# A three-block fp32 model on one core: modulation vectors by rows, convolution taps from PSUM, and other moves in the first block

## The chip, the cores and the metric

The program runs on one core of one Trainium2 chip. The metric is the device time of one execution in microseconds (us); lower is better. Before the change the median of three runs is 3274.16 us (3274.14 to 3275.22).

## What is computed

Three blocks in a chain act on x, 512 tokens by 1024 features, all in fp32. Only the first block changes. Cut to what matters here:

```
m_x = (silu(c) @ w_mod + b_mod)            # six vectors of 1024: shift, scale, gate, shift, scale, gate
m_c = (silu(c_ctx) @ w_mod + b_mod)
hc  = modulate(ctx, m_c[0], m_c[1]);  hx = modulate(x, m_x[0], m_x[1])     # rmsnorm, scale, shift
px  = hx @ w_in                            # columns: recurrent input 1280, gelu gate 1280, u, v, two gates
xr  = depthwise conv over time, 4 taps, of (ctx part, x part)
y_lru = RG-LRU both ways over ctx + x, 5 heads of 256: r, i = sigmoid(xr @ wa), sigmoid(xr @ wx)
        a = exp(-c softplus(lam) r);  h = a h + sqrt(1 - a*a) (i xr);  forward + backward
y_r = gelu(px gate) * y_lru;   y_g = u * (w_s v + b_s)
merged = sigmoid(gate_r) * (y_r @ w_pr) + sigmoid(gate_g) * (y_g @ w_pg)
x = x + m_x[2] * (merged @ w_out)
x = x + m_x[5] * conv_ffn(modulate(x, m_x[3], m_x[4]))
```

The second block begins with `silu(c_2) @ w_ada + b_ada`, three more vectors of 1024, which the first block computes on the side.

## The kernel before

**Products.** Each fp32 product is made of three passes: weight and activation are both split into a rounded high part and a low rest, and `dense` issues high by high (L419), high by low (L420) and low by high (L422) into one PSUM bank; `dense_n` (L438 to L440) is the same with the roles swapped. Activations stand as features by tokens, 128 features to a tile and 512 tokens (256 for ctx) to a row.

**Weights.** `Stream` brings all large weights in chunks of eight 128x128 tiles (512 KB) in the order in which they are used. SP loads a chunk into `wst` (two buffers, L99), then ACT (L102) or DVE (L104) casts it to the high part `whi`, by the letter that `hi_pattern` has for the chunk ("a" is ACT, "v" is DVE), and DVE subtracts for the low part `wlo` (L107). `whi` and `wlo` have rings of six buffers: chunk n can be cast only when PE is through with chunk n − 6.

**Start (`block1`).** x and ctx are loaded, the first 2048 columns of w_mod go through PE as 32 tiles `wm` of 256 KB (`gemv` inside `block1`), and x and ctx are normed and modulated.

**Recurrent part (`lru`).** For each of five heads: the convolution's input product for the next head into two banks (px for x, pc for ctx), its four taps (`conv_taps`), and for either direction the gates (`gates`): products into a PSUM tile `pair`, tanh on ACT (L866), exp and tanh of a (L871, L872), a*a on DVE (L873), the square root on ACT (L879), and the scan along time on DVE (L884 forward, L887 backward). The taps first copy px and pc to SBUF on ACT (L836, L837) into tiles with zeroed borders (Pool memsets); the first tap is a DVE tensor_scalar (L841), the others DVE scalar_tensor_tensor operations. That operation is issued by a helper, so every one of them has line L549.

**Mixer (`mixer1`).** Four loops over output tiles: u (8, with the chunk products L950 to L955), t1 (8), yr (10) and the merge loop (8), then w_out in `final_stage`: four output tiles at full width, then the other four in halves of 256 tokens. Each is closed by an epilogue on DVE, `xh<-mm,gate,s` (out = PSUM times gate plus residual), which frees the PSUM bank. Four banks carry the tag "mm" and are used in turn.

**Modulation vectors on the side (`gemv`, `column`).** The other 32 column groups of w_mod and the 24 of w_ada are computed on DVE: 14 blocks of eight tiles 128x512 (256 KB, four buffers `gv`), each tile scaled by a column of silu(c) and added up (L687 and L549), and after each block four small matmuls with ones on PE (L673) that add over the partitions. The blocks stand between the output tiles of the t1, yr and merge loops.

**Bias matrices (`toeplitz`).** A small table is expanded to `tmat` in DRAM, 4 MB written by two transfers on SP's queue ahead of the u loop; the second block reads it.

The program is written with a tile scheduler, which sets the order of the instructions on each engine; an engine then runs its own in that order and waits for what each needs.

Of the kernel before, what the change touches and what calls it, by code (L numbers as in the profile page):

```python
# [11 lines left out]
AF = mybir.ActivationFunctionType  # L12
OP = mybir.AluOpType
# [3 lines left out]
P = 128  # L17
D = 1024
KD = D // P
T = 512  # L20
# [354 lines left out]
class Kernel:  # L375
# [299 lines left out]
    def gemv(self, new, src, nblk, cs, out, bias):  # L675

        nc = self.nc
        prev = None
        for b in list(range(nblk)) + [None]:
            acc = None  # L680
            if b is not None:
                acc = new()
                for k in range(KD):
                    st = new()
                    nc.sync.dma_start(st, src[b][k])
                    if k == 0:
                        nc.vector.tensor_scalar(acc, st, cs[:, 0:1], None, op0=OP.mult)  # L687
                    else:
                        self.stt(acc, st, cs[:, k:k + 1], acc, OP.mult, OP.add)
            if prev is not None:  # L690
                ps = self.sd()
                self.column(ps, prev)
                o = slice(4 * b - 4, 4 * b) if b is not None else slice(4 * nblk - 4, 4 * nblk)
                nc.vector.tensor_add(out[:, o], ps[:, :4], bias[:, o])
            prev = acc
            yield
# [5 lines left out]
    def block1(self, es):  # L702
        nc, S, ai, cp, mod = self.nc, self.S, self.ai, self.cpool, self.mod
        with ExitStack() as b1:
# [8 lines left out]
            with ExitStack() as st:  # L713
# [4 lines left out]
                S.hi_pattern = "v"  # L718
# [11 lines left out]
                cs2 = cs.rearrange("p (a k) -> p k a", a=2)  # L730

                def gemv(i, b, at={}):
# [3 lines left out]
                    for k in range(KD):  # L736
                        wm = self.t(p0, [P, T], "wm", bufs=12)
                        nc.sync.dma_start(wm, ai["wmod01"][i][k])
                        if i < 2 and k % 2 == 0:
                            j = 4 * i + k // 2  # L740
                            nc.sync.dma_start(x[j], ai["xT"][j])
                            nc.sync.dma_start(ctx[j], ai["ctxT"][j])
                            nx.square("q", j, FULL)
                            ncx.square("q", j, ncols)
# [38 lines left out]
                t = gemv(2, 1, {0: t, 2: columns})  # L783
# [4 lines left out]
            S.hi_pattern = "v"  # L788
# [6 lines left out]
    def lru(self, hx, hc, s1c):  # L795
# [8 lines left out]
        with ExitStack() as es:  # L804
# [25 lines left out]
            def conv_taps(m, px, pc, xr, xs):  # L830
                bx = self.t(p, [P, T + 4], "bx", bufs=2)
                bc = self.t(p, [P, TC + 4], "bc", bufs=2)
                for b, n in ((bx, T), (bc, TC)):
                    nc.gpsimd.memset(b[:, 0:2], 0.0)
                    nc.gpsimd.memset(b[:, n + 2:n + 3], 0.0)
                nc.scalar.copy(bx[:, 2:T + 2], px)  # L836
                nc.scalar.copy(bc[:, 2:TC + 2], pc[:, :TC])  # L837
                r = self.t(p, [P, TC + T + TC], "xr", bufs=4)
                for b, n, o in ((bc, TC, 0), (bx, T, TC)):
                    dst = r[:, o:o + n]  # L840
                    nc.vector.tensor_scalar(dst, b[:, 0:n], self.v("cw1", m), self.v("cb1", m),  # L841
                                            op0=OP.mult, op1=OP.add)
                    for j in range(1, 4):
                        self.stt(dst, b[:, j:j + n], self.v("cw1", 10 * j + m), dst, OP.mult, OP.add)
# [7 lines left out]
            def gates(h, d, xr, xs, y):  # L852

                ax, ac = xs.view(slice(TC, N)), xs.view(slice(0, TC))
                q = self.t(p, [P, 2, N], "q", bufs=1)
                aa, bb = [], []
                for mt in range(2):
# [15 lines left out]
                    nc.vector.tensor_mul(q[:, mt, :], a, a)  # L873
# [6 lines left out]
                for mt in range(2):  # L880
                    nc.vector.tensor_mul(bb[mt], bb[mt], q[:, mt, :])
                    f = q[:, mt, :]
                    if d == 0:
                        nc.vector.tensor_tensor_scan(f, aa[mt], bb[mt], 0.0, op0=OP.mult, op1=OP.add)  # L884
                        nc.vector.tensor_copy(y[mt], f[:, TC:N])
                    else:
                        nc.vector.tensor_tensor_scan(f[:, ::-1], aa[mt][:, ::-1], bb[mt][:, ::-1], 0.0,  # L887
                                                     op0=OP.mult, op1=OP.add)
                        nc.vector.tensor_add(y[mt], y[mt], f[:, 0:T])
# [15 lines left out]
            for h in range(5):  # L905
                y = [self.xh() if 2 * h + i < 8 else self.t(self.s0, [P, T], f"y{2 * h + i}") for i in range(2)]
                nr, ns = [], Act()
                for d in range(2):
# [4 lines left out]
                    gates(h, d, xr, xs, y)  # L913
# [12 lines left out]
    def mixer1(self, hx, ylru, vt):  # L926
        nc, ai, cp, mod, cs = self.nc, self.ai, self.cpool, self.mod, self.cs
        with ExitStack() as es:
# [9 lines left out]
            self.toeplitz(slot)  # L938
            yg = Act()
            for m in range(8):  # L940
                pu = self.mm()
# [17 lines left out]
            gn = lambda: self.t(s2, [P, T], "gv", bufs=4)  # L959
            gv = self.gemv(gn, ai["wmod25"], 8, cs, mod[:, 16:48], self.v("b_mod", 16, 32))  # L960
            t1 = []
            for m in range(8):
# [4 lines left out]
                nc.scalar.activation(tg, pg, AF.Tanh, scale=0.5)  # L967
                self.dense("w_pg", m * P, KD, [(pp, yg)])
# [4 lines left out]
            for m in range(10):  # L973
                pr = self.mm()
                self.dense("w_in", 1280 + m * P, KD, [(pr, hx)])
# [6 lines left out]
                if m == 0:  # L982
                    next(gv)
            cs2 = self.t(self.s0, [P, 8], "cs_2")
            nc.scalar.activation(cs2, self.v("c2", 0, 8), AF.Silu)
            gv = self.gemv(gn, ai["wada"], 6, cs2, self.ada, self.v("b_ada", 0, 24))
            mg = Act()
            for m in range(8):
                pg, pp = self.mm(), self.mm()
                if m < 7:  # L990
                    next(gv)
                self.dense("w_in", 4608 + m * P, KD, [(pg, hx)])
                tg = tt()
                nc.scalar.activation(tg, pg, AF.Tanh, scale=0.5)
                self.dense("w_pr", m * P, 10, [(pp, yr)])
# [94 lines left out]
    def toeplitz(self, alloc):  # L1090
# [4 lines left out]
        nc.sync.dma_start(tab, self.ai["t5"])  # L1095
        for i in range(2):
            oh = alloc()[:33, :320]
            nc.sync.dma_start(oh, self.ai["onehot"][i])
# [4 lines left out]
            nc.sync.dma_start(self.trow[:, i * 320:(i + 1) * 320], row)  # L1103
        self.tmat = self.t(self.dpool, [16, P, T], "tmat")
        for r in range(0, 16, 8):
            src = self.trow[r:r + 8, 0:T]
            if not isinstance(src, Mock):
                src = bass.AP(tensor=src.tensor, offset=src.offset + 127, ap=[[640, 8], [-1, P], [1, T]])
            nc.sync.dma_start(self.tmat[r:r + 8], src)
# [873 lines left out]
```

## Time and profile before

| | |
|---|---|
| median of three runs | 3274.16 us |
| the profiled execution | 3279.36 us |
| span of its records | 3277.6 us |
| mean granted clock of PE | 0.988 |
| matmuls | 15534, 97% of the span busy |
| bytes moved | 352.52 MB, 108 GB/s on average |

The profile gives for every engine the busy time, and for an engine that sat idle what released it. The parts of the program can be told apart by time: start 0 to 45 us, recurrent part to 237, u loop to about 350, t1 and yr loops to about 490, merge loop to about 600, w_out to about 640, and then the first block's FFN and the other two blocks, whose instructions the change leaves as they are.

### The profile page before, as it was taken

To read this page: it belongs to the slowest core of one execution; us is meant where nothing else is said; L and a number is where in the kernel's file an instruction comes from. 1 tells how busy PE (TensorE), PEld (TensorE's weight loads), DVE (VectorE), ACT (ScalarE), POOL (GpSimd) and SP (SyncE) were. 2 spreads that over 40 slices of the span, in tenths; PEclk is the share of its full clock that TensorE was granted. 3 is DMA by queue.
4 is the path that set the end of the run, shared out by engine and by line. 5 is a ranking of instruction groups with operands and counts; after the bars stand their busy time and mean duration, and the time that the engine had idled before them with its cause. 6 is when DMAs were issued, how large, how long until landed. Compare 5 with 4: busy or idle time off the path is not lost.

```text
span 3277.6 us, 40053 instructions
## 1 busy us (share of the span) xinstructions
PE 3187.5 (97%) x15534; PEld 2639.8 (81%) x15534; DVE 2035.1 (62%) x3160; ACT 1310.2 (40%) x2010; POOL 193.6 (6%) x268
## 2 busy tenths in 40 slices
PE   8999999999999999999999999999899999989998
PEld 4778788888888888888887888888877787878887
DVE  6997676588837756655787353333796747563334
ACT  4665232344424444333665233222543535342222
POOL 2100000100001000000000010000200012020001
PEclk9999999999999999999999999999999999999999
DMA  5114776423333232222232333333323131333331
GB/s 204 52 58 134 238 223 199 140 90 97 106 113 105 78 90 84 84 90 85 74 97 74 110 116 103 103 106 106 117 75 124 61 105 61 122 103 97 106 109 62
DMA packets 123108, 352.52 MB, mean 108 GB/s; under 512 B 13978, under 2 KB 28668, under 8 KB 122788
## 3 DMA queue, kind: packets, MB, share of 16 engines
q1 hardware_dynamic: 118612, 336.18, 32.6%
q0 software_dynamic: 4304, 13.77, 1.3%
q8 instruction: 122, 2.00, 0.2%
q14 instruction: 70, 0.57, 0.1%
HBM read 337.27 MB, written 16.82 MB: 108 GB/s over the span
## 4 chain that ended last, share of the span: by engine, by line
PE 80%; DVE 11%; DMA 3%; issue 3%; ACT 2%; SPq 0%; POOL 0%; ACTq 0%; DVEq 0%; POOLq 0%
PE mm L420 19%; PE mm L419 19%; PE mm L422 18%; PE sd L420 4%; PE sd L422 4%; PE sd L419 4%; PE mm L440 2%; PE mm L439 2%; PE mm L438 2%; DVE wlo L107 2%; DMA gv<-in_wmod 2%; DVE xh L549 1%; PE sd L495 1%; PE sd L496 1%; PE sd L497 1%
## 5 line engine op out<-in xcount | busy, mean ns | idle before, releaser
L107 DVE TENSOR_TENSOR wlo<-wst,whi 128x1024 fp32r<-128x1024 f32 x496 | 609.4, 1230 | 614.7 <-ACT whi L102 605.5
L102 ACT CAST whi<-wst 128x1024 fp32r<-128x1024 f32 x485 | 509.1, 1051 | 1174.8 <-PE mm L420 732.5
L420 PE MATMUL mm<-xh,whi 128*128 128x512 f32 (+1 forms) x2256 | 857.5, 381 | 16.0 <-DVE xh L549 11.9
L419 PE MATMUL mm<-xh,whi 128*128 128x512 f32 (+1 forms) x2256 | 857.2, 381 | 14.5 <-ACT xh L364 10.5
L422 PE MATMUL mm<-xh,wlo 128*128 128x512 f32 (+1 forms) x2256 | 849.7, 379 | 0.0
L420 PEld LDWEIGHTS mm<-xh,whi 128*128 128x128 f32 x2256 | 430.4, 191 | 94.6 <-DVE xh L549 16.1
L419 PEld LDWEIGHTS mm<-xh,whi 128*128 128x128 f32 x2256 | 429.8, 191 | 94.5 <-ACT xh L364 11.4
L422 PEld LDWEIGHTS mm<-xh,wlo 128*128 128x128 f32 x2256 | 428.3, 191 | 74.0 <-issue 2.9
L419 PE MATMUL sd<-xh,whi 128*128 128x512 f32 (+1 forms) x576 | 215.2, 374 | 0.0
L420 PE MATMUL sd<-xh,whi 128*128 128x512 f32 (+1 forms) x576 | 214.6, 372 | 0.0
L422 PE MATMUL sd<-xh,wlo 128*128 128x512 f32 (+1 forms) x576 | 214.5, 372 | 0.0
L420 PE MATMUL mm<-d,whi 128*128 128x512 f32 (+1 forms) x540 | 187.7, 348 | 0.0
L422 PE MATMUL mm<-d,wlo 128*128 128x512 f32 (+1 forms) x540 | 187.2, 347 | 0.0
L419 PE MATMUL mm<-d,whi 128*128 128x512 f32 (+1 forms) x540 | 187.1, 347 | 0.0
L438 PE MATMUL mm<-whi,xh 128*128 128x512 f32 x336 | 131.7, 394 | 6.1 <-DVE whi L104 3.1
L439 PE MATMUL mm<-wlo,xh 128*128 128x512 f32 x336 | 132.8, 395 | 0.6 <-DVE wlo L107 0.6
L440 PE MATMUL mm<-whi,xh 128*128 128x512 f32 x336 | 132.0, 394 | 0.0
L549 DVE SCALAR_TENSOR_TENSOR t<-t,vec,t 128x441 f32<-128x441 f32 (+2 forms) x176 | 122.7, 701 | 9.6 <-ACT t L1046 5.3
L419 PEld LDWEIGHTS sd<-xh,whi 128*128 128x128 f32 x576 | 109.5, 190 | 18.8
L420 PEld LDWEIGHTS sd<-xh,whi 128*128 128x128 f32 x576 | 109.2, 190 | 18.8
L422 PEld LDWEIGHTS sd<-xh,wlo 128*128 128x128 f32 x576 | 109.2, 190 | 18.7
L1510 DVE TENSOR_TENSOR t<-t,sd 128x512 f32<-128x512 f32 x44 | 30.2, 688 | 144.7 <-PE sd L422 141.1
(482 smaller groups left out, 5187.6 us busy)
## 6 DMA issues: line engine op xcount, KB each, us to landing
wst<-in_w SPq DMA_DIRECT2D x516, 512.0 KB, 3.6
gv<-in_wmod SPq DMA_DIRECT2D x64, 256.0 KB, 3.5
gv<-in_wada SPq DMA_DIRECT2D x48, 256.0 KB, 3.5
t<-xd POOLq DMA_DIRECT2D x40, 256.0 KB, 3.6
xd<-xh SPq DMA_DIRECT2D x72, 128.0 KB, 1.8
wm<-in_wmod SPq DMA_DIRECT2D x32, 256.0 KB, 5.0
tmat<-trow SPq DMA_DIRECT2D x2, 2048.0 KB
tp<-tmat SPq DMA_DIRECT2D x16, 256.0 KB, 2.6
```

The source lines that it names most:

```text
L102: self.after(nc.scalar.copy(hi, st))
L107: self.after(eng.tensor_sub(lo, st, hi.bitcast(FT)))
L419: mm(ps, wh, a.hi[k], start=(k == 0), stop=False)
L420: mm(ps, wh, a.lo[k], start=False, stop=False)
L422: mm(ps, wl, a.hi[k], start=False, stop=(k == K - 1))
L438: mm(ps, a.hi[k][:, s], wh, start=(k == 0), stop=False)
L439: mm(ps, a.hi[k][:, s], wl, start=False, stop=False)
L440: mm(ps, a.lo[k][:, s], wh, start=False, stop=(k == K - 1))
L495: mm(ps, l[0], r[0], start=start, stop=False)
L496: mm(ps, l[0], r[1], start=False, stop=False)
L497: mm(ps, l[1], r[0], start=False, stop=stop)
L549: self.nc.vector.scalar_tensor_tensor(out, in0, s, in1, op0=op0, op1=op1)
```

## The change

1. **Modulation vectors by rows.** w_mod and w_ada are stored transposed. One tile is 128 columns of the matrix by 1024 inputs (512 KB, two buffers `gv`), and one DVE tensor_tensor_reduce (L681 of the changed kernel) multiplies it by silu(c), held in all 128 partitions (`cb`, one buffer, loaded on Pool's queue, Silu on ACT), and adds along the row. 56 tiles take the place of 14 blocks of eight; the small matmuls go. Two tiles stand beside each output tile of the u loop from the second on, two in t1, one in yr, two in the merge loop.
2. **Taps from PSUM.** ACT writes the tap of weight index 2 straight from PSUM with scale and bias; the three others are DVE operations that read PSUM. The copies, the borders and the memsets go.
3. **Gates.** a*a becomes an ACT Square; the buffer q has three copies instead of one; the forward result is no longer copied, since the backward add reads it in q.
4. **Casts.** At the start all high parts are cast on ACT instead of DVE, in the recurrent part every second one.
5. **Start.** x and ctx are loaded behind the weight tiles 0, 2, 5, 7, 10, 12, 15 and 17 instead of every second one of the first 16; the norm's columns come later.
6. **Bias matrices.** All their transfers go to Pool's queue, and `tmat` is written in eight pieces, most of them in the yr loop.

```diff
-    def gemv(self, new, src, nblk, cs, out, bias):
+    def gemv(self, new, src, n, cb, out, bias):
 
         nc = self.nc
-        prev = None
-        for b in list(range(nblk)) + [None]:
-            acc = None
-            if b is not None:
-                acc = new()
-                for k in range(KD):
-                    st = new()
-                    nc.sync.dma_start(st, src[b][k])
-                    if k == 0:
-                        nc.vector.tensor_scalar(acc, st, cs[:, 0:1], None, op0=OP.mult)
-                    else:
-                        self.stt(acc, st, cs[:, k:k + 1], acc, OP.mult, OP.add)
-            if prev is not None:
-                ps = self.sd()
-                self.column(ps, prev)
-                o = slice(4 * b - 4, 4 * b) if b is not None else slice(4 * nblk - 4, 4 * nblk)
-                nc.vector.tensor_add(out[:, o], ps[:, :4], bias[:, o])
-            prev = acc
+        for j in range(n):
+            st = new()
+            nc.sync.dma_start(st, src[j])
+            nc.vector.tensor_tensor_reduce(out=st, in0=st, in1=cb, op0=OP.mult, op1=OP.add, scale=1.0, scalar=0.0,
+                                           accum_out=out[:, j:j + 1])
+            if j == n - 1:
+                nc.vector.tensor_add(out, out, bias)
             yield
...
-                S.hi_pattern = "v"
+                S.hi_pattern = "a"
...
+                at_x = (0, 2, 5, 7, 10, 12, 15, 17)
...
-                        if i < 2 and k % 2 == 0:
-                            j = 4 * i + k // 2
+                        if 8 * i + k in at_x:
+                            j = at_x.index(8 * i + k)
...
-                t = gemv(2, 1, {0: t, 2: columns})
+                t = gemv(2, 1, {0: t, 1: nx.warm, 5: columns})
...
-            S.hi_pattern = "v"
+            S.hi_pattern = "av"
...
             def conv_taps(m, px, pc, xr, xs):
-                bx = self.t(p, [P, T + 4], "bx", bufs=2)
-                bc = self.t(p, [P, TC + 4], "bc", bufs=2)
-                for b, n in ((bx, T), (bc, TC)):
-                    nc.gpsimd.memset(b[:, 0:2], 0.0)
-                    nc.gpsimd.memset(b[:, n + 2:n + 3], 0.0)
-                nc.scalar.copy(bx[:, 2:T + 2], px)
-                nc.scalar.copy(bc[:, 2:TC + 2], pc[:, :TC])
                 r = self.t(p, [P, TC + T + TC], "xr", bufs=4)
-                for b, n, o in ((bc, TC, 0), (bx, T, TC)):
-                    dst = r[:, o:o + n]
-                    nc.vector.tensor_scalar(dst, b[:, 0:n], self.v("cw1", m), self.v("cb1", m),
-                                            op0=OP.mult, op1=OP.add)
-                    for j in range(1, 4):
-                        self.stt(dst, b[:, j:j + n], self.v("cw1", 10 * j + m), dst, OP.mult, OP.add)
+                for ps, n, o in ((pc, TC, 0), (px, T, TC)):
+                    nc.scalar.activation(r[:, o:o + n], ps[:, :n], AF.Identity, bias=self.v("cb1", m),
+                                         scale=self.v("cw1", 20 + m))
+                for j in (1, 3, 0):
+                    d = j - 2
+                    for ps, n, o in ((pc, TC, 0), (px, T, TC)):
+                        dst = r[:, o + max(0, -d):o + n - max(0, d)]
+                        self.stt(dst, ps[:, max(0, d):n - max(0, -d)], self.v("cw1", 10 * j + m), dst, OP.mult, OP.add)
...
-            def gates(h, d, xr, xs, y):
+            def gates(h, d, xr, xs, y, fwd):
 
                 ax, ac = xs.view(slice(TC, N)), xs.view(slice(0, TC))
-                q = self.t(p, [P, 2, N], "q", bufs=1)
+                q = self.t(p, [P, 2, N], "q", bufs=3)
...
-                    nc.vector.tensor_mul(q[:, mt, :], a, a)
+                    nc.scalar.activation(q[:, mt, :], a, AF.Square)
...
-                        nc.vector.tensor_copy(y[mt], f[:, TC:N])
...
-                        nc.vector.tensor_add(y[mt], y[mt], f[:, 0:T])
+                        nc.vector.tensor_add(y[mt], fwd[:, mt, TC:N], f[:, 0:T])
...
-            self.toeplitz(slot)
+            toeplitz = self.toeplitz(slot)
+            next(toeplitz)
+            gn = lambda: self.t(s2, [P, D], "gv", bufs=2)
+
+            def columns():
+                for name, w, n, out, b in (("c_b", "wmod25", 32, mod[:, 16:48], self.v("b_mod", 16, 32)),
+                                           ("c2_b", "wada", 24, self.ada, self.v("b_ada", 0, 24))):
+                    cb = self.t(s2, [P, D], "cb")
+                    nc.gpsimd.dma_start(cb, ai[name])
+                    nc.scalar.activation(cb, cb, AF.Silu)
+                    yield from self.gemv(gn, ai[w], n, cb, out, b)
+
+            gv = columns()
             yg = Act()
             for m in range(8):
+                if m:
+                    next(gv)
...
-            gn = lambda: self.t(s2, [P, T], "gv", bufs=4)
-            gv = self.gemv(gn, ai["wmod25"], 8, cs, mod[:, 16:48], self.v("b_mod", 16, 32))
...
+                next(gv)
                 self.dense("w_pg", m * P, KD, [(pp, yg)])
...
+                next(toeplitz, None)
                 self.dense("w_in", 1280 + m * P, KD, [(pr, hx)])
...
-                if m == 0:
-                    next(gv)
-            cs2 = self.t(self.s0, [P, 8], "cs_2")
-            nc.scalar.activation(cs2, self.v("c2", 0, 8), AF.Silu)
-            gv = self.gemv(gn, ai["wada"], 6, cs2, self.ada, self.v("b_ada", 0, 24))
+                next(gv)
             mg = Act()
             for m in range(8):
                 pg, pp = self.mm(), self.mm()
-                if m < 7:
-                    next(gv)
+                next(gv)
                 self.dense("w_in", 4608 + m * P, KD, [(pg, hx)])
                 tg = tt()
                 nc.scalar.activation(tg, pg, AF.Tanh, scale=0.5)
+                next(gv)
                 self.dense("w_pr", m * P, 10, [(pp, yr)])
...
-        for r in range(0, 16, 8):
-            src = self.trow[r:r + 8, 0:T]
+        yield
+        for r in range(0, 16, 2):
+            src = self.trow[r:r + 2, 0:T]
             if not isinstance(src, Mock):
-                src = bass.AP(tensor=src.tensor, offset=src.offset + 127, ap=[[640, 8], [-1, P], [1, T]])
-            nc.sync.dma_start(self.tmat[r:r + 8], src)
+                src = bass.AP(tensor=src.tensor, offset=src.offset + 127, ap=[[640, 2], [-1, P], [1, T]])
+            nc.gpsimd.dma_start(self.tmat[r:r + 2], src)
+            yield
```

### The order around the change

Names carry buffer numbers: `wlo89` is the low part of weight chunk 89, `mm_659` and so on are PSUM tiles, and the number behind the last underscore is the program's own counter.

DVE before, from the last chunks of the merge loop into w_out (four epilogues `xh<-mm,gate2,s` at full width):

```order
L107 TENSOR_TENSOR wlo86_5034<-wst86_5030,whi86_5032 128x1024
L549 SCALAR_TENSOR_TENSOR xh_737_4892<-mm_761_4916,gate2_735_4888,s_763_4978 128x512
L107 TENSOR_TENSOR wlo87_5077<-wst87_5073,whi87_5075 128x1024
L549 SCALAR_TENSOR_TENSOR xh_738_4893<-mm_762_4917,gate2_735_4888,s_765_4984 128x512
L207 TENSOR_TENSOR s_764_4982<-s_764_4982,s_766_4988 128x512
L549 SCALAR_TENSOR_TENSOR xh_739_4894<-mm_767_4991,gate2_735_4888,s_768_5022 128x512
L107 TENSOR_TENSOR wlo88_5114<-wst88_5110,whi88_5112 128x1024
L207 TENSOR_TENSOR s_764_4982<-s_764_4982,s_769_5026 128x512
L549 SCALAR_TENSOR_TENSOR xh_740_4895<-mm_770_5029,gate2_735_4888,s_771_5060 128x512
L107 TENSOR_TENSOR wlo89_5151<-wst89_5147,whi89_5149 128x1024
L207 TENSOR_TENSOR s_764_4982<-s_764_4982,s_772_5064 128x512
```

The casts' low parts and the epilogues alternate; the operations on `gv` stand far above these rows, between the tiles of the merge loop. DVE in the changed kernel, the same place:

```order
L107 TENSOR_TENSOR wlo86_4692<-wst86_4688,whi86_4690 128x1024
L107 TENSOR_TENSOR wlo87_4735<-wst87_4731,whi87_4733 128x1024
L107 TENSOR_TENSOR wlo88_4772<-wst88_4768,whi88_4770 128x1024
L107 TENSOR_TENSOR wlo89_4809<-wst89_4805,whi89_4807 128x1024
L681 ISA gv_541_3582,ada_48_116<-gv_541_3582,cb_540_3579 128x1024
L681 ISA ada_48_116 128x1
L681 ISA gv_546_3624,ada_48_116<-gv_546_3624,cb_540_3579 128x1024
...
L681 ISA gv_630_4500,ada_48_116<-gv_630_4500,cb_540_3579 128x1024
L684 TENSOR_TENSOR ada_48_116<-ada_48_116,vec_4_69 128x24
L549 SCALAR_TENSOR_TENSOR gs_2_840_6930<-ada_48_116,vec_4_69 128x8
L1140 TENSOR_SCALAR gate_2_1852_14953<-ada_48_116 128x8
L1084 TENSOR_TENSOR gs_2_840_6930<-gs_2_840_6930,vec_4_69 128x8
L549 SCALAR_TENSOR_TENSOR xh_635_4550<-mm_659_4574,gate2_633_4546,s_661_4636 128x512
```

The 24 reductions of w_ada (each an instruction on 128x1024 and one that reads its sum) stand in one run behind `wlo89`, with nothing between them, and the first epilogue of w_out stands behind the last of them. ACT in the changed kernel, where the factor of these reductions is made:

```order
L102 CAST whi86_4690<-wst86_4688 128x1024
L102 CAST whi87_4733<-wst87_4731 128x1024
L102 CAST whi88_4770<-wst88_4768 128x1024
L102 CAST whi89_4807<-wst89_4805 128x1024
L932 ACT_TABLE_LOAD
L932 ACTIVATE cb_540_3579<-cb_540_3579 128x1024
L203 ACTIVATE s_662_4640<-xh_635_4550 128x512
```

The Silu for the second vector (L932) stands behind the cast of chunk 89 and ahead of the first square of the next norm. PE in the changed kernel, where w_out goes from full width to halves:

```order
L419 MATMUL mm_668_4687<-s_631_4542,whi83_4578 128x512
L420 MATMUL mm_668_4687<-s_632_4543,whi83_4578 128x512
L422 MATMUL mm_668_4687<-s_631_4542,wlo83_4580 128x512
L419 MATMUL mm_671_4725<-hc_582_3961,whi84_4608 128x256
L420 MATMUL mm_671_4725<-hc_583_3962,whi84_4608 128x256
L422 MATMUL mm_671_4725<-hc_582_3961,wlo84_4610 128x256
```

The last full-width tile uses chunk 83; the first half-width matmul writes `mm_671`, the fifth "mm" tile from `mm_659` on (`mm_659`, `mm_660`, `mm_665`, `mm_668`, `mm_671`), and so the bank of `mm_659`, which the first epilogue reads. On SP, 22 of the 24 loads of w_ada stand in one row behind the load of chunk 91 and ahead of that of chunk 92; before, they stood between the weights.

## Rows read from the trace of the kernel before

**Rows 1.** Part 1 of the page: for each engine busy us (share of the span) x instructions.

```profile
PE 3187.5 (97%) x15534; PEld 2639.8 (81%) x15534; DVE 2035.1 (62%) x3160; ACT 1310.2 (40%) x2010; POOL 193.6 (6%) x268
```

**Rows 2.** The table by windows: stretch of the span in us, its length, then for each engine busy us (x instructions), the granted clock of PE, the busy share of the DMA engines and GB/s.

```profile
core 0: us, PE busy (x) PEld busy (x) DVE busy (x) ACT busy (x) POOL busy (x), PEclk, DMA share, GB/s
0.00:20.00 20.00, 12.96 (x26) 1.95 (x26) 4.93 (x19) 7.76 (x17) 0.20 (x4) 1.00 0.93 320
20.00:40.00 20.00, 18.82 (x58) 5.03 (x59) 9.19 (x26) 6.02 (x13) 0.91 (x2) 1.00 0.98 354
140.00:190.00 50.00, 47.38 (x261) 40.60 (x261) 48.69 (x64) 31.44 (x34) 8.89 (x11) 0.97 0.16 50
152.40:193.10 40.70, 38.08 (x207) 32.44 (x206) 39.39 (x52) 25.98 (x28) 4.34 (x10) 0.96 0.17 53
300.00:480.00 180.00, 175.39 (x812) 141.83 (x811) 121.57 (x191) 51.05 (x68) 0.00 (x0) 0.99 0.69 225
480.00:620.00 140.00, 140.00 (x634) 114.96 (x632) 78.81 (x108) 39.61 (x50) 4.49 (x8) 1.00 0.59 184
620.00:640.00 20.00, 20.00 (x166) 19.86 (x165) 10.79 (x17) 8.11 (x13) 0.73 (x1) 1.00 0.30 99
640.00:660.00 20.00, 15.42 (x100) 14.34 (x100) 18.63 (x30) 7.94 (x18) 7.03 (x3) 0.83 0.32 101
830.00:900.00 70.00, 70.00 (x311) 57.95 (x310) 57.43 (x77) 29.64 (x39) 1.62 (x3) 1.00 0.35 109
```

**Rows 3.** The chain of waits, pieces in order of time: start us, length us, what. Two pieces of the recurrent part, and one block of eight ones-matmuls for w_mod and one for w_ada (on the chain there are five of the first kind, 1.02 to 1.07 us, and six of the second, all 0.79).

```profile
155.23 1.22 PE pair L419 x2
195.90 1.22 PE pair L419 x2
372.22 1.07 PE sd L673 x8
572.43 0.79 PE sd L673 x8
```

**Rows 4.** Groups of instructions on DVE in the stretch 152.4 to 193.1 us, one head: line, engine, operation, out<-in, shape, count | busy us, mean ns of one | idle before.

```profile
L549 DVE SCALAR_TENSOR_TENSOR xr<-bx,vec,xr 128x512 f32<-128x512 f32 x6 | 4.4, 741 | 0.0
L873 DVE TENSOR_TENSOR q<-a 128x768 f32<-128x768 f32 x4 | 3.8, 954 | 0.0
L104 DVE CAST whi<-wst 128x1024 fp32r<-128x1024 f32 x3 | 2.0, 683 | 0.0
L841 DVE TENSOR_SCALAR xr<-bx,vec 128x512 f32<-128x512 f32 x2 | 1.1, 536 | 0.0
L841 DVE TENSOR_SCALAR xr<-bc,vec 128x256 f32<-128x256 f32 x2 | 0.8, 405 | 0.0
L885 DVE COPY xh<-q 128x512 f32<-128x512 f32 x2 | 0.7, 412 | 0.0
```

**Rows 5.** The same on ACT.

```profile
L871 ACT ACTIVATE a<-tg,cof 128x768 f32<-128x768 f32 x4 | 4.1, 1035 | 0.1
L866 ACT ACTIVATE tg<-pair,hbx 128x768 f32<-128x768 f32 x4 | 3.6, 901 | 1.5 <-DVE q L549 1.3 <-DVE q L884 0.2
L866 ACT ACT_TABLE_LOAD x2 | 2.6, 1283 | 3.7 <-PE pair L422 3.7
L836 ACT COPY bx<-mm 128x512 f32<-128x512 f32 x2 | 1.2, 587 | 0.8 <-PE mm L422 0.8
```

**Rows 6.** Part 5 of the page, all of the span: the casts of the weights' high parts on ACT.

```profile
L102 ACT CAST whi<-wst 128x1024 fp32r<-128x1024 f32 x485 | 509.1, 1051 | 1174.8 <-PE mm L420 732.5
```

**Rows 7.** Groups on DVE from 300 to 640 us: operations that read PSUM.

```profile
L549 DVE SCALAR_TENSOR_TENSOR s<-t,mm 128x512 f32<-128x512 f32 x8 | 5.5, 685 | 6.6 <-PE mm L422 6.6
L549 DVE SCALAR_TENSOR_TENSOR t<-t,mm 128x512 f32<-128x512 f32 x8 | 5.5, 683 | 6.3 <-PE mm L422 6.3
L549 DVE SCALAR_TENSOR_TENSOR xh<-mm,gate,s 128x512 f32<-128x512 f32 x4 | 3.0, 750 | 6.4 <-PE mm L422 6.4
```

**Rows 8.** Groups on DVE over the whole span: the scaling and adding of the tiles of w_mod and w_ada.

```profile
L549 DVE SCALAR_TENSOR_TENSOR gv<-gv,cs,gv 128x512 f32<-128x512 f32 x98 | 73.4, 749 | 62.2 <-DMA gv<-in_wmod 33.1 <-DMA gv<-in_wada 28.2
L687 DVE TENSOR_SCALAR gv<-gv,cs 128x512 f32<-128x512 f32 x14 | 6.8, 483 | 7.3 <-DMA gv<-in_wada 6.1 <-DMA gv<-in_wmod 1.2
```

**Rows 9.** Groups on DVE over the whole span: fused multiply-and-reduce operations of the second block by row length, and the reading of their sums.

```profile
L1365 DVE CUSTOM_DVE_ANT_0 sm<-sd,tp 128x384 f32<-128x384 f32 x16 | 8.2, 550 | 0.0
L1365 DVE CUSTOM_DVE_ANT_0 sm<-sd,tp 128x512 f32<-128x512 f32 x16 | 10.8, 675 | 0.0
L1365 DVE DVE_READ_ACCUMULATOR2_ANT nm<- 128x1 f32 x96 | 8.0, 83 | 0.0
```

**Rows 10.** Groups from 300 to 640 us: the ones-matmuls on PE, and on DVE the small addition of a bias behind them.

```profile
L673 PE MATMUL sd<-ones,gv 128*128 128x1 f32 x112 | 13.9, 245 | 2.2 <-DVE gv L549 2.0
...
L694 DVE TENSOR_TENSOR ada<-sd,vec 128x4 f32<-128x4 f32 x6 | 0.9, 157 | 0.1
```

**Rows 11.** Timelines around the start of the half-width tiles of w_out: start us, length us, engine, line, operation; first PE, then DVE.

```profile
620.47 0.28 PE L419 MATMUL mm<-hc,whi 128*128 128x256 f32 x1
...
620.67 0.75 DVE L549 SCALAR_TENSOR_TENSOR xh<-mm,gate,s 128x512 f32<-128x512 f32 x1 [2.92 <-PE mm L422]
```

**Rows 12.** DMA issues, out<-in, queue, count, KB each, median us from issue to landing: a quiet stretch (700 to 900 us), then 320 to 650 us.

```profile
wst<-in_w SPq DMA_DIRECT2D x37, 512.0 KB, 3.5
...
wst<-in_w SPq DMA_DIRECT2D x56, 512.0 KB, 4.1
```

More of the change, by code (lines that the diff above doesn't have):

```diff
@@ L888, in gates @@
                                                      op0=OP.mult, op1=OP.add)
-                        nc.vector.tensor_add(y[mt], y[mt], f[:, 0:T])
+                        nc.vector.tensor_add(y[mt], fwd[:, mt, TC:N], f[:, 0:T])
+                return q
             def values(nb, sums):
@@ L906, in lru @@
                 y = [self.xh() if 2 * h + i < 8 else self.t(self.s0, [P, T], f"y{2 * h + i}") for i in range(2)]
-                nr, ns = [], Act()
+                nr, ns, fwd = [], Act(), None
                 for d in range(2):
@@ L912, in lru @@
                         values(d, sums)
-                    gates(h, d, xr, xs, y)
+                    fwd = gates(h, d, xr, xs, y, fwd)
                     if h < 4:
@@ L994, in mixer1 @@
                 nc.scalar.activation(tg, pg, AF.Tanh, scale=0.5)
+                next(gv)
                 self.dense("w_pr", m * P, 10, [(pp, yr)])
@@ L1094, in toeplitz @@
         tab = alloc()[:33, :16]
-        nc.sync.dma_start(tab, self.ai["t5"])
+        nc.gpsimd.dma_start(tab, self.ai["t5"])
         for i in range(2):
             oh = alloc()[:33, :320]
-            nc.sync.dma_start(oh, self.ai["onehot"][i])
+            nc.gpsimd.dma_start(oh, self.ai["onehot"][i])
             ps = self.sd()
@@ L1102, in toeplitz @@
             nc.scalar.activation(row, ps[0:16, :320], AF.Copy, scale=8.0)
-            nc.sync.dma_start(self.trow[:, i * 320:(i + 1) * 320], row)
+            nc.gpsimd.dma_start(self.trow[:, i * 320:(i + 1) * 320], row)
         self.tmat = self.t(self.dpool, [16, P, T], "tmat")
-        for r in range(0, 16, 8):
-            src = self.trow[r:r + 8, 0:T]
+        yield
+        for r in range(0, 16, 2):
+            src = self.trow[r:r + 2, 0:T]
             if not isinstance(src, Mock):
-                src = bass.AP(tensor=src.tensor, offset=src.offset + 127, ap=[[640, 8], [-1, P], [1, T]])
-            nc.sync.dma_start(self.tmat[r:r + 8], src)
+                src = bass.AP(tensor=src.tensor, offset=src.offset + 127, ap=[[640, 2], [-1, P], [1, T]])
+            nc.gpsimd.dma_start(self.tmat[r:r + 2], src)
+            yield
     def load_toeplitz(self, dst, r):
@@ L1931, in layout @@
     arrays["wmod01"] = np.ascontiguousarray(wm[:, :, :2048].reshape(KD, P, 4, T).transpose(2, 0, 1, 3)[[0, 2, 1, 3]])
-    arrays["wmod25"] = np.ascontiguousarray(wm[:, :, 2048:].reshape(KD, P, 8, T).transpose(2, 0, 1, 3))
-    arrays["wada"] = np.ascontiguousarray(g["w_ada_2"][0].reshape(KD, P, 6, T).transpose(2, 0, 1, 3))
+    arrays["wmod25"] = np.ascontiguousarray(g["w_mod"][0][:, 2048:].T).reshape(32, P, D)
+    arrays["wada"] = np.ascontiguousarray(g["w_ada_2"][0].T).reshape(24, P, D)
+    arrays["c_b"] = np.ascontiguousarray(np.broadcast_to(g["c"].reshape(1, D), (P, D)))
+    arrays["c2_b"] = np.ascontiguousarray(np.broadcast_to(g["c_2"].reshape(1, D), (P, D)))
     arrays["bs_b"] = np.ascontiguousarray(np.broadcast_to(g["b_s"][0].T[:, None, :], (8, P, P)))
```

## The prediction

> **What bounds the kernel now.** I read the page's engine shares first. TensorE (PE) is busy 97% of the span, VectorE (DVE) 62%, ScalarE (ACT) 40% [rows 1], so over the whole program only what stops or feeds PE counts. The table by windows then shows the exceptions inside the first block [rows 2]. In its first 40 us the DMA engines are busy .93 to .98: the start is paced by loading. From 140 to 190 us DVE is busy 48.69 of 50 us and PE loses time: that is the recurrent part. From 480 to 620 us, the merge loop, PE is busy 140.00 of 140 and DVE only 78.8: there DVE has room, and PE sets the pace.
>
> **The recurrent part.** One head issues 96 matmuls of 512 columns and 96 of 256 (convolution 48 and 48, gates 48 and 48). Back to back they take 70.00/311 = .225 us and 20.00/166 = .120 us [rows 2], so PE needs 33.1 us. The chain of waits gives the real period: the gates' first matmul waits for ACT's xs_h split at 155.23 and at 195.90 [rows 3], 40.67 us apart. DVE is busy 39.39 and ACT 25.98 of such a stretch [rows 2]: DVE is the bound.
> The change takes from DVE per head the squares of a (3.8), the copies of y (.7), the first taps (1.1 + .8) and, with every second weight cast on ACT, half of the 2.0 for casts: 7.4 us [rows 4], which leaves 32.0. It gives ACT four squares at about 1.0 us (a 128x768 activation takes 1.03) and two casts of 1.05, and swaps its copies from PSUM (.59 at 512 columns) for scaled copies of the same shapes (nothing) [rows 5, 6]: 25.98 + 6.2 = 32.2. PE needs 33.1. The most this can give is 40.67 − 33.1 = 7.6 us a head, 30 us over the four heads with a convolution beside the gates. The least is 0: three engines at 32 to 33 us each, in fixed orders that wait for one another, need not run side by side. I take the middle, **−15 us**. The Pool memsets go too, and cost nothing, as POOL is busy 4.34 of 40.7 [rows 2].
> The six taps per m-tile now read PSUM. In the trace a DVE operation of this kind with a PSUM operand took 683 to 685 ns, or 750 with a column of factors, at 512 columns; the taps from SBUF took 741 [rows 4, 7]. I therefore book no extra. [...] What remains is that the taps hold the PSUM bank until the last of them, which is a reason for the middle and not the upper end.
>
> **The modulation vectors.** Before, 112 tiles of 256 KB cost DVE 73.4 + 6.8 us [rows 8], beside PE work; after, 56 reductions over 1024 columns. The nearest rows are the reductions L1365: 550 ns at 384 columns and 675 at 512, so .125 per 128 columns, 1.18 to 1.2 us at 1024, plus .083 to read the sum [rows 9]: 1.28 us, 72 us in all. In the u, t1 and yr loops DVE has room (121.6 of 180 us busy [rows 2]), so the 32 reductions there cost nothing; without that cover each would cost its 1.28.
> The ones-matmuls of `column` go off PE: 13.9 us busy and 2.0 of waits for DVE [rows 10]. The ends of their records overlap the next matmuls; by the pieces of the chain, 8 blocks at up to 1.07 and 6 at .79 [rows 3], they hold PE for 13 us. **−15 us** with the waits.
>
> **Where the last 24 reductions stand.** This decides the result. Their factor cb is one buffer for both vectors, and its second Silu stands in ACT's order behind the cast of weight chunk 89. In DVE's order all 24 reductions stand in one run behind that chunk's wlo, and the first epilogue of w_out stands behind all 24. Chunk 89 takes the ring slot of chunk 83, so the cast waits until PE has finished chunk 83, the last full-width m-tile. PE's next instruction, the first half-width matmul, needs the PSUM bank that this first epilogue frees. So PE stops at the end of chunk 83 (620.47 us in the profile before, where the epilogue ran .2 us later [rows 11]) until DVE is through. Queued behind the run on DVE are all epilogues, wlo of chunk 90 and the second block's factors; PE waits for the first of them.
> The wait: cast 1.05, table load 1.28 and Silu about 1.1 before the first reduction [rows 5, 6], 3.4. There are two gv buffers and 22 of the 24 loads stand in a row on SP's queue; each waits for the reduction two before it. 512 KB land in 3.5 us median [rows 12], so two reductions take 3.5 + 1.28 = 4.8 us: 11 × 4.8 + 2 × 1.28 = 55.4. Then four small operations at .16 (.65) and the epilogue .75 [rows 7, 10]. **+60.2 us.** Bounds: 24 × 1.28 + 4.8 = 35.5 if loads kept up with DVE; at 4.1-us landings, as between 320 and 650 us [rows 12], 66.8. [...]
> After a stop PE's clock falls: around the stalls at 640 to 660 us .83 was granted over 20 us [rows 2], 3.4 us lost. **+3.4 us** (0 to 3.4).
>
> **Edits at nothing.** x loaded between more weights at the start: bytes and queue are the same, and DMA is the bound there: 0, with −4 to +4 kept, as x's last tiles come later than before. tmat in 8 pieces on Pool's queue: SP no longer carries 4 MB ahead of the u loop's loads, but PE idled only 4.6 of 180 us from 300 to 480 [rows 2]: 0, −4 to +4; were Pool's queue late, the residual loads behind it would be late next.
>
> **Sum.** 60.2 + 3.4 − 15 − 15 = **+33.6 us**. On the profiled execution (3279.36; span 3277.6) that gives 3313.0; the median of the three runs is 5.2 lower, 3274.16, and gives **3307.8**.
>
> **Rivals.**
> - *Faster: the reductions run at DVE's pace.* If 512 KB landed in time for a reduction every 1.28 us, the stop would be 35.5, the clock would not matter, and with the upper gains (30 + 15 + 4) the time would be 3274.2 + 35.5 − 49 = 3261. It decides at a landing of 2.5 us: 3.4 + 2.6 + 11 × 3.8 + 1.4 = 49. For it: from 620 to 640 us the DMA share is only .30 [rows 2]. Against: even so the median landing in quiet stretches is 3.5 [rows 12]. Chance .05.
> - *The change doesn't do what it seems to:* DVE gets into the run of reductions well before PE has finished chunk 83, and the merge loop hides it, as it hid the 48 operations before. Then the gains alone are left, 3274 − 30 = 3244. Against: wlo and cast of chunk 89 stand ahead, and a ring of six lets neither start. Chance .03.
> - *The recurrent part gives nothing,* because ACT takes DVE's place (its tanh reads PE and its square root DVE, and it already waits on both [rows 5]): +48.6, 3323. Chance .17.
> - *Slower loads:* 4.1 us each, stop 66.8, and PE late on the weights queued behind the 22 loads or in the u loop, up to 8: 3314 to 3322, and with no gain in the recurrent part and 4 lost at the start, up to 3339. Chance .13.
>
> **How the numbers follow.** My forecast has .62. Its own lower end is the 60-us stop with all gains: 60 − 49 = +11, without the clock's 3.4, and about 3281 with landings at 3.1. The upper end is 3339 from the last rival. I give 3281 to 3339; out of it lie the two faster cases (.08) and tails on either side. A measurement of this kernel can tell about .2%, 6.5 us, from no change. Faster .08, same .03, slower .89.
>
> **What would show it.** Right: one PE stop of 55 to 67 us at about 590 to 625 us, released by the DVE epilogue; under it 24 reductions in pairs every 4.8 us waiting for DMA gv; no L673 with gv; the period of a head between 33 and 40 us. Wrong: reductions between the merge loop's wlo, a pitch near 1.3 us, or a period of 40 us or more with ACT at 95%.

## The result, and the profile after

The changed kernel takes 3321.27 us in the median (3318.74 to 3326.12 in four runs) against 3274.15 before: a ratio of 1.0145, 95% interval 1.0127 to 1.0163. That is 47 us slower; 33.6 us more were forecast, 3307.8 us, in a range of 3281 to 3339. The profiled execution has a span of 3324.3 us, 46.7 more than before.

The table by windows of the changed kernel, columns as in [rows 2]; the first row is one head of the recurrent part:

```profile
core 0: us, PE busy (x) PEld busy (x) DVE busy (x) ACT busy (x) POOL busy (x), PEclk, DMA share, GB/s
107.44:141.03 33.59, 33.59 (x193) 29.19 (x193) 32.03 (x39) 31.31 (x34) 0.80 (x2) 1.00 0.20 60
300.00:480.00 180.00, 174.30 (x764) 142.83 (x765) 101.88 (x151) 53.71 (x70) 5.90 (x6) 0.98 0.66 208
600.00:620.00 20.00, 0.00 (x0) 0.00 (x0) 9.42 (x15) 0.00 (x0) 0.00 (x0) 0.50 0.63 195
640.00:660.00 20.00, 0.00 (x0) 0.00 (x0) 9.40 (x19) 0.00 (x0) 0.00 (x0) 0.50 0.52 160
660.00:680.00 20.00, 19.50 (x144) 19.29 (x144) 7.85 (x13) 5.68 (x9) 0.00 (x0) 0.87 0.20 73
```

Two things are to be seen: in a head all three engines are nearly full, PE without a gap; and there are windows in which PE does nothing at all. PE's waits from 240 to 760 us (tile and line that waited, what for: us, times, longest) name the largest:

```profile
PE mm L419 <- DVE xh L549: 69.2, 2, 68.3
PE sd L950 <- DMA wsT<-in_wsT: 5.8, 3, 4.1
```

The chain of waits through that stop (start us, length us, what), to its third pair of loads and at its end:

```profile
593.10 1.28 ACT L932
594.39 1.06 ACT cb L932
595.48 1.23 DVE gv L681
596.71 1.14 DVE gv L681
597.89 4.38 DMA gv<-in_wada
602.40 1.23 DVE gv L681
603.66 4.09 DMA gv<-in_wada
607.89 1.22 DVE gv L681
...
653.49 4.30 DMA gv<-in_wada
657.93 1.23 DVE gv L681
659.78 0.67 DVE xh L549
660.50 0.58 PE mm L419
```

After table load, Silu and two reductions the chain alternates: a load of 4.2 us, a reduction of 1.23. From 602.40 to 657.93 there are ten steps, 5.55 us each, of two reductions each.

The factor cb of these reductions was on the chip long before. Pool's issue of its load (start us, time in the issue, line):

```profile
395.94 0.59 POOL L931 DMA_DIRECT2D cb<-in_c_b  x1 [102.08 <-DVE mod L684]
```

It landed 7.8 us later, at about 404 us; the Silu that ACT's order has behind the cast of chunk 89 began at 594.39. The stop comes from the order as built and not from a factor that came late.

To see where the time went, the same matmul is taken in both traces (the products of `dense` and `dense_n`, counted from the last one back) and its start times, from the start of each span, are subtracted. After minus before, with the times before; this is the matmul table of the text below:

| start before, us | place | after − before | step |
|---|---|---|---|
| 43.77 | first product | −1.5 | −1.5 |
| 75.16 | first gates | +0.4 | +1.9 |
| 300.09 | u loop begins to wait | −21.3 | −21.7 |
| 320.17 | u loop | −12.1 | +9.2 |
| 598.07 | merge loop done | −28.4 | −16.3 |
| 620.47 | first half-width tile of w_out | +40.0 | +68.4 |
| 690.03 | FFN | +44.2 | +4.2 |
| 2100.16 | third block | +43.5 | −0.7 |
| 3200.06 | near the end | +46.5 | +3.0 |

### The profile page after: what moved, and what is told of

Its sections match the earlier page's. It is cut to its first block, busy times and chain, and to the rows that moved or that the text cites. A ratio compares the mean times of both kernels' runs of the same rounds, so it can differ in the third digit from the quotient of the medians.

```text
span 3324.3 us, 39583 instructions
## 1 busy us (share of the span) xinstructions
PE 3168.4 (95%) x15422; PEld 2625.0 (79%) x15422; DVE 1986.4 (60%) x3082; ACT 1349.0 (41%) x2051; POOL 183.9 (6%) x243
## 4 chain that ended last, share of the span: by engine, by line
PE 84%; DVE 8%; DMA 4%; ACT 2%; issue 2%; POOL 0%; SPq 0%; ACTq 0%; DVEq 0%; POOLq 0%
PE mm L420 19%; PE mm L419 19%; PE mm L422 19%; PE sd L420 4%; PE sd L422 4%; PE sd L419 4%; PE mm L438 2%; PE mm L440 2%; PE mm L439 2%; DMA gv<-in_wada 1%; DVE wlo L107 1%; DVE xh L549 1%; PE sd L495 1%; PE sd L496 1%; PE sd L497 1%
## 5 line engine op out<-in xcount | busy, mean ns | idle before, releaser
L102 ACT CAST whi<-wst 128x1024 fp32r<-128x1024 f32 x501 | 525.9, 1051 | 1199.2 <-PE mm L420 737.9
```

Of the source, the lines that this page charges most:

```text
L102: self.after(nc.scalar.copy(hi, st))
```

## The experiments

All ratios are against the kernel before, run beside them on the same chip (its own median there was 3272 to 3276 us).

### e1: cb on SP's queue

```diff
-                    nc.gpsimd.dma_start(cb, ai[name])
+                    nc.sync.dma_start(cb, ai[name])
```

> The changed kernel with one edit: the two loads of cb go on SP's queue instead of Pool's. In the order this spreads the 24 reductions of w_ada over the yr and merge loops; Pool's queue then issues its eight tmat pieces in one run at the start of the u loop. Theory (the stop at w_out comes from the place of the run of reductions alone, and that from cb standing behind tmat on Pool's queue): no PE stop over 3 us at w_out, 3321.3 - 68.4 - 4 for the clock after it = 3249, with 0 to 10 us more where the tmat pieces crowd the u loop: 3246 to 3262. Rival (DVE or the loads can't carry the reductions there and the time comes back spread over the loops): 3290 or more.

Measured: 3263.84 us, ratio 0.9958 (0.9943 to 0.9973). The stop is gone and the reductions stand between the tiles. The first line is of PE's waits from 590 to 640 us, the second the reading of the sums of w_ada (times in ns, then first and last start in us):

```profile
PE mm L419 <- DVE xh L549: 3.8, 2, 2.8
L681 DVE DVE_READ_ACCUMULATOR2_ANT ada<- x24: 81/83/85, 410.2 to 474.5; 128x1 f32 x24
```

So the theory holds for the 68 us as far as the place of the run goes, and the rival falls. That tmat on the same queue is the reason why cb was ordered so late is not shown by itself: no run moves tmat and leaves cb. One line, the queue of two loads, is worth 57 us. The total is 1.8 us above the upper end of what was expected, and two places show why. PE waits for wsT twice as long as in the changed kernel, and Pool's queue now has seven tmat pieces in one run (7.45 us of issues from 288.76, where the changed kernel has three in 3.22); PE's waits from 280 to 345 us:

```profile
PE sd L950 <- DMA wsT<-in_wsT: 11.9, 2, 7.8
```

and the window of the crowd, columns as above:

```profile
290.00:320.00 30.00, 18.07 (x80) 15.27 (x80) 15.08 (x36) 6.91 (x11) 7.28 (x7) 0.75 1.01 281
```

The DMA engines are full and .75 of PE's clock is granted. By the matmul table the u loop costs 13.8 us here from 300 to 350 us, against 8.7 in the changed kernel. The second place is w_out: its first epilogue stands behind wlo of chunk 89 in DVE's order, and PE waits 2.8 us for it.

### e2: the same run of reductions without its loads

```diff
         for j in range(n):
-            st = new()
-            nc.sync.dma_start(st, src[j])
+            if n == 32 or j < 2:
+                st = new()
+                nc.sync.dma_start(st, src[j])
...
-                nc.vector.tensor_add(out, out, bias)
+                nc.vector.tensor_add(out, out if n == 32 else bias, bias)
```

> The changed kernel without 22 of the 24 loads of w_ada: the reductions multiply the two tiles that are there over and over, and the three vectors of the second block are replaced by a constant, so that part of the computation is left out. The run of 24 reductions stays where it is. Theory (the loads set the pitch of the run, 5.6 us for two): the stop falls to 3.4 + 24 x 1.31 + 1.4 = 36 us and the time to 3321.3 - 32 = 3289 (3284 to 3294). Rival (the pitch is DVE's own or that of the waits between engines): stop 60 us or more, 3313 or more.

Measured: 3289.81 us in one run, as the theory has it; PE's stop is 34.8 us. Groups on DVE from 590 to 628 us:

```profile
L682 DVE CUSTOM_DVE_ANT_0 gv<-gv,cb 128x1024 f32<-128x1024 f32 x24 | 29.3, 1224 | 1.9 <-ACT cb L933 1.1
L682 DVE DVE_READ_ACCUMULATOR2_ANT ada<- 128x1 f32 x24 | 2.0, 82 | 0.0
```

24 reductions in a row take 31.3 us. So of the 68.3 us of the stop, 33.5 are waiting for loads; the rest is the work of DVE and the Silu ahead of it, which PE must wait for because the run stands where it does.

### e3: the recurrent part's edits alone, in the kernel before

```diff
-            S.hi_pattern = "v"
+            S.hi_pattern = "av"
             ylru, vt = self.lru(hx, hc, s1c)
... (conv_taps, gates and the calls of gates in lru as in the change; nothing else)
```

> The kernel before with the edits of the recurrent part alone (taps from PSUM, Square on ACT, three q, no copy of y, every second cast on ACT). Theory (the 21 us gained between 43 and 260 us come from these): head period 33.6 us, 3274.2 - 21 = 3253 (3250 to 3257). Rival (part of it is the start's: other casts and x loaded otherwise): gain of 14 or less, 3260 or more.

Measured: 3271.03 us, ratio 0.9984 (0.9975 to 0.9994), 5 us in place of 21. The theory's total missed. The number fits the rival, but its reason does not: by the matmul table this kernel gains 21.2 us from the first gates to 300 us, nearly all of the changed kernel's 21.7, and by 350 it has lost 12.8 of them again. Three of the waits from 280 to 330 us:

```profile
DVE t L949 <- DMA bsb<-in_bs_b: 17.8, 1, 17.8
PEld sd L945 <- DMA wsT<-in_wsT: 12.7, 1, 12.7
PE sd L945 <- DMA wsT<-in_wsT: 12.2, 1, 12.2
```

and SP's queue (start us, time in the issue, line):

```profile
290.60 5.71 SPq L1104 DMA_DIRECT2D tmat<-trow  x2
296.41 10.77 SPq L941 DMA_DIRECT2D bsb<-in_bs_b  x2
307.27 1.19 SPq L942 DMA_DIRECT2D wsT<-in_wsT  x2
```

The small loads of the u loop stand behind the 4 MB of tmat, and PE comes to wsT before SP is through. So the gain of the recurrent part reaches the total only if the u loop's loads don't wait for tmat.

### e4: cb and tmat on SP's queue

```diff
-            nc.gpsimd.dma_start(self.tmat[r:r + 2], src)
+            nc.sync.dma_start(self.tmat[r:r + 2], src)
... (and cb as in e1)
```

> As e1, and the eight tmat pieces on SP's queue too, where the first stands behind the loads of the u loop. Theory A (the 9 us lost in the u loop come from tmat written on Pool's queue while the u loop's small loads and weights are wanted): the u loop is back to its time before and the total 8 to 12 under e1's, 3236 to 3250. Rival B (the reductions' own loads, 512 KB each ahead of wsT and the weights on SP's queue, cost it): within 4 us of e1.

Measured: 3295.18 us, ratio 1.0059 (1.0044 to 1.0074), 31 over e1; both expectations for the total miss. The u loop is as theory A has it (at 350 us 23.6 ahead, 1.9 more than at 300). But from 400 to 510 us 44 are lost: PE waits 29.4 us for casts of weights that come late. SP's queue there:

```profile
435.76 0.62 SPq L1106 DMA_DIRECT2D tmat<-trow  x1
436.49 11.75 SPq L99 DMA_DIRECT2D wst<-in_w  x1
448.28 0.59 SPq L680 DMA_DIRECT2D gv<-in_wada  x1
448.92 0.63 SPq L1106 DMA_DIRECT2D tmat<-trow  x1
449.66 9.51 SPq L99 DMA_DIRECT2D wst<-in_w  x1
```

Behind each of the last five pieces of 512 KB the next weight chunk sits 9.5 to 11.8 us in its issue. Behind the first three the next issues took 6.4 us at most. In the kernel before, the two pieces of 2 MB held the next load once, for 10.4 us.

### e5, e6, e7: tmat in the FFN; reductions from t1 on

```diff
-            toeplitz = self.toeplitz(slot)
-            next(toeplitz)
...
+            toeplitz = self.toeplitz(tt)
             def tail(m, pg, pu):
+                if m >= 4:
+                    next(toeplitz, None)
```

e5 is this on top of e1, on Pool's queue in eight pieces; e6 has it on SP's queue in two; e7 is e6 with no reduction in the u loop and three beside each tile of t1, two in yr, two in the first six of the merge loop.

> As e1 (cb on SP's queue), and the whole making of the bias matrices moved from the start of the u loop into the first block's FFN, in eight pieces on Pool's queue. Theory (the u loop's 15 us in e1, and the 3 us at w_out whose epilogues stood behind wlo of chunk 89, both come from tmat on Pool's queue in the mixer): PE waits under 3 us for wsT, the epilogues run beside PE, 3264 - 18 = 3246 (3243 to 3251). Rival (the reductions' loads in the u loop cost it): 3256 or more.

> As e5, with the bias matrices on SP's queue in two pieces of 2 MB, as in the kernel before, but in the FFN. In e4 a piece of 512 KB held SP's queue for 10 to 12 us; in the kernel before a piece of 2 MB held it for about as long. Theory: two such holds of SP's queue are covered there by the weight chunks that are ahead; within 3 us of e5. Rival: PE waits for weights in the FFN, 10 us or more above e5.

> As e6, and no reduction in the u loop: three beside each tile of t1, two in yr, two in the first six of the merge loop. Theory (with tmat gone the u loop carries its 14 reductions at nothing): within 3 us of e6. Rival (their loads still delay wsT and the weights there): 4 to 9 us under e6.

Measured: e5 3247.70 us, ratio 0.9928 (0.9911 to 0.9946); e6 3247.89, 0.9921 (0.9907 to 0.9936); e7 3249.52, 0.9929 (0.9914 to 0.9944); all three totals as their theories have it. PE's waits in e5 from 240 to 680 us are now:

```profile
PE mm L420 <- DVE xh L549: 4.2, 3, 2.9
PE mm L419 <- ACT s L500: 2.3, 1, 2.3
PE sd L948 <- DVE hc L549: 0.3, 2, 0.2
```

No wait for wsT is left, and none for the first epilogue. The u loop's loss was tmat's: from 300 to 350 us e5 gains 1.4 us by the matmul table, where e1 lost 13.8. The 14 reductions there cost under 1 us: e7 without them is .8 better than e6 up to 350 us, and 3.9 worse from there to the end of the merge loop, where it has more of them. These versions beat the kernel before, run beside them, by 25.7 to 27.5 us, and are only a few small moves away from the changed one.

The bias matrices are not free in the FFN either. In e6 PE waits once 5.0 us for a cast, and 7.1 us are lost there. ACT at the end of that wait:

```profile
715.79 0.62 ACT L500 CAST d<-t 128x512 fp32r<-128x512 f32 x1 [0.76 <-DVE t L1047]
716.32 1.99 ACT L102 CAST whi<-wst 128x1024 fp32r<-128x1024 f32 x2
```

From 700 to 710 us no DMA moved anything (0 GB/s), so these casts were not waiting for a transfer: on ACT they run right behind L500, an operation of the FFN. SP's queue had been held once behind the two pieces, 10.3 us from 677.91, and was by then itself waiting for the buffers of these casts. That the order came out so because of the bias matrices is argued and not shown. e5, with them on Pool's queue, has no such wait, but loses 4.8 us near 950 us of the kernel before; the cause of that was not looked for.

### e8 to e11: what the gain of the recurrent part is made of

Each is e7 with one thing put back, or e9 for the last; one run each.

```diff
-                    nc.scalar.activation(q[:, mt, :], a, AF.Square)                 # e8
+                    nc.vector.tensor_mul(q[:, mt, :], a, a)
-                q = self.t(p, [P, 2, N], "q", bufs=3)                               # e9, e11
+                q = self.t(p, [P, 2, N], "q", bufs=2)
-            S.hi_pattern = "av"                                                     # e10
+            S.hi_pattern = "v"
... (e11 has conv_taps of the kernel before)
```

> As e7, with a*a back on DVE. In the changed kernel a head takes 33.55 us with DVE busy 32.0 of 33.59, ACT 31.3 and PE all of it. Theory A (DVE's work per head is what set the period of the kernel before): DVE goes to 32.0 + 3.8 = 35.8, the period to 36 or a little more, and of the 21 us gained in the recurrent part 9 to 12 go, 3259 to 3262. Rival B (the buffers, not the work, set it): the period stays under 34.5.

> As e7, with two q buffers instead of three. Theory A (work): period 33.6, unchanged, 3250. Rival B (the forward result that stays in q holds the next direction up): period 35 or more, 3255 or more.

> As e7, with all of the recurrent part's casts on DVE again. Theory A: DVE 32.0 + 1.4 = 33.4 beside PE's 33.55, so a period of 33.6 to 34.6 and 0 to 4 us lost. Rival (the order of the weights' casts matters more than DVE's sum): period over 35.

> As e9 (two q, since three don't fit beside the copies), with the taps of the kernel before: copies to SBUF on ACT and four taps on DVE. Theory A: DVE 32.0 + 1.9 = 33.9 a head, ACT's scaled copies turn back into copies (-0.6); period 34 to 35, 2 to 6 us over e9. Rival (reading PSUM costs the taps what the copies would): period as in e9.

The last column is the gain over the kernel before from the first gates (75.16 us) to 300 us. The changed kernel, e1, e2 and e4 to e7 have the same recurrent part and agree in it, 21.6 to 21.7 us; the totals are less exact, as e7 ran on another chip than e8 to e11 (the kernel before took 3275.2 us beside e7 and 3271.8 beside those).

| | time, us | periods of heads 2 and 3, us | gained by 300 us |
|---|---|---|---|
| before | | 39.9, 38.2 | 0 |
| e7 | 3249.5 | 33.6, 33.6 | 21.6 |
| e8 | 3255.7 | 34.9, 34.2 | 15.3 |
| e9 | 3251.1 | 33.6, 33.6 | 21.6 |
| e10 | 3251.4 | 33.6, 34.2 | 20.7 |
| e11 | 3253.8 | 34.5, 35.5 | 17.6 |

Squares are worth 6.3 us, less than theory A's 9 to 12; the taps 4.0 (e9 minus e11); the casts .9; the third q nothing. Theory A holds for e9, e10 and, but for half a microsecond in one period, e11. In e8 neither side's numbers came: the periods are under A's 36, and one is over B's 34.5. None alone brings the old period back. The table by windows, columns as above, for heads 2 and 3 of the kernel before and then of e8:

```profile
107.42:147.33 39.91, 36.52 (x194) 31.46 (x193) 37.86 (x50) 25.22 (x27) 1.88 (x6) 0.91 0.18 54
147.33:185.54 38.21, 35.59 (x195) 30.32 (x193) 36.90 (x47) 25.98 (x28) 4.33 (x10) 0.96 0.18 55
106.84:141.75 34.91, 33.83 (x195) 29.19 (x193) 34.80 (x43) 28.61 (x30) 2.27 (x2) 1.00 0.17 52
141.75:175.97 34.22, 34.02 (x194) 29.15 (x193) 34.12 (x42) 28.83 (x30) 1.97 (x2) 1.00 0.18 56
```

In e8 DVE idles .1 us of a head, so its work sets the period there, as theory A has it, at a lower price than one to one. In the kernel before, DVE idles 2.05 and 1.31 us. That single q buffer, which no run here tries, can have cost about that much at most; the rest of the 4.6 to 6.3 us over PE's 33.6 is DVE's work. That the edits together make up the old period is a sum of such parts and was not run the other way round; the copy of y was not put back by itself.

## Why the prediction was right, step by step

The mechanism came as forecast: one stop of PE at w_out, made by the place of 24 reductions, with the loads setting its length. The number was 13.5 us too low, and that it was no more is luck: the stop was 8 us longer than forecast, the u loop lost 9 that were booked at nothing, and a gain in the recurrent part 7 us over the forecast hid part of that. In its sizes the result is the rival *Slower loads*, which had .13: loads of 4.1 us, a stop of 66.8, up to 8 lost in the u loop, 3314 to 3322. (The upper end of that rival adds up to 3341, not 3339.) The sign that was to show the forecast right, a stop of 55 to 67 us in pairs of 4.8, was missed by a little on both counts. The rival in which the recurrent part gives nothing had 3323, as near to the measured time; it falls by the period of a head, 33.6 us.

- **The stop** was the deciding step and stands where it was put: behind chunk 83, until the first epilogue, with the 24 reductions in pairs. It is 68.3 us, from 592 to 660 us, and not 60.2. The term that was too small is the pair of loads: 5.55 us instead of 4.8, because a load took 4.2 us and not the 3.5 of [rows 12]; 11 × .75 = 8.2. DMA issues from 592 to 660 us:

```profile
gv<-in_wada SPq DMA_DIRECT2D x22, 512.0 KB, 4.2
wst<-in_w SPq DMA_DIRECT2D x1, 512.0 KB, 3.5
```

  By their issues and landings two of these loads were in flight in 29.0 of the 61 us from the first issue to the last landing; that the second makes the first slower was not tried by itself. A reduction took 1.22 to 1.23 us plus .083, against the 1.28 drawn from [rows 9]. The landing of 3.1 us that goes with the forecast's lower end, 3281, is shown neither before nor after: the shortest load of a 512 KB weight chunk took 3.3 us in both traces, the shortest of these 22 took 3.5.
- **The clock after it**: PE stood at a granted clock of .50 in the stop and was granted .87 from 660 to 680 us, 2.6 us lost of the 3.4 booked. By the matmul table 4.2 us are lost from the end of the stop to 690 us, other waits included.
- **The recurrent part**: −21.7 instead of −15. DVE 32.03 and ACT 31.31 a head were forecast as 32.0 and 32.2 (on ACT two errors cancel: a Square took .83 us and not 1.0, a scaled copy from PSUM .77 at 512 columns and not the .59 of a plain one). The step that failed is the choice of the middle: three engines at 31 to 33.6 us did run side by side, and the heads reached PE's pace (33.55 against 33.1). Yet the gain was not the 30 us of the upper end, because 40.67 is not the period of a head: it is the distance of two waits on the chain. From first gates to first gates the heads before took 34.5, 39.9 and 38.2 us, and 57.5 with other products in the fourth; after, 33.6, 33.6, 33.5 and 47.0. That leaves some 22 us to gain, and they were gained. The two errors, a ceiling too high and half of it taken, work against each other. The taps from PSUM cost what the taps from SBUF did: 740 ns at 511 columns against 741 at 512 [rows 4], and 470 at 255 against 474 at 256. Groups on DVE from 107.44 to 141.03 us, then one of the kernel before from 152.4 to 193.1:

```profile
L549 DVE SCALAR_TENSOR_TENSOR xr<-mm,vec,xr 128x511 f32<-128x511 f32 x4 | 3.0, 740 | 0.0
L549 DVE SCALAR_TENSOR_TENSOR xr<-mm,vec,xr 128x255 f32<-128x255 f32 x4 | 1.9, 470 | 0.0
...
L549 DVE SCALAR_TENSOR_TENSOR xr<-bc,vec,xr 128x256 f32<-128x256 f32 x6 | 2.8, 474 | 0.0
```

- **The vectors off PE**: −16.3 from the u loop to the end of the merge loop, against −15. From 350 us to there the changed kernel gains 15.8, and e3, which keeps the old vectors, 2.1; so some 14 of them are the vectors'.
- **Edits at nothing**: the start came out at +0.4. The u loop did not: +9.2, over the 4 that were kept for tmat. The step booked tmat as covered because PE idled little there before; e3 shows that the cover was the slow recurrent part, and e1 and e5 together that the cost is tmat's.
- **The rest**: 3 us between 2100 us and the end, where the order is the same, were not forecast and stay open; e1 and e6 lose about 2 there too and get 1.6 of them back, e3 loses .2.

## What to carry to other kernels

When a load goes to another engine's queue, look at what it then stands behind in the built order, and what stands behind it: one queue choice was worth 57 us here, more than the rest of the change gained. The run of loads through two buffers cost landing plus use for every two, 5.55 us with a landing of 4.2 and a use of 1.23 on the chain; the landing that fitted was that of this stretch and not the 3.5 of a quiet one. A period has to be taken between two like places of the loop, not between two waits. A stall saved ahead of a transfer that the stall had hidden came back as a wait for the transfer: in e3, 12.8 of 21.2 us.

## Not expected of the hardware

A transfer of 512 KB out of the small overlapping table (tmat) held what stood behind it on SP's queue 9.5 to 11.8 us five times in e4, while a weight chunk of the same size landed in 3.5 to 4.1 in the kernel before [rows 12]. In the kernel before, two pieces of 2 MB held the next load 10.4 us, and in e6 10.3. Fewer, larger pieces were cheaper for the queue here.
